# Differential attention in a two-layer trunk: the bias table written reversed for every partition, the softmax turned to minima, one division moved into the output norm

## The chip, the cores and the metric

The kernel runs on one core of a Trainium2 chip. The metric is the device time of one execution in microseconds (us); of several runs the median counts. Inside the core, TensorE (PE) multiplies matrices, VectorE (DVE), ScalarE (ACT) and GpSimd (POOL) work on elements, and SyncE (SP) issues transfers. ACT and POOL issue transfers as well. Every engine takes its instructions in order, and semaphores make one wait for another.

## The reference, cut to what matters

The kernel computes a trunk of two layers on 512 tokens of width 1024: a Mamba-2 mixer, a feed-forward block with a short convolution (FFN 0), a differential attention with a relative-position bias, and a second feed-forward block (FFN 1). The change is in the attention and in the table of its bias:

```python
dist = qpos[:, None] - kpos[None, :]
bias = rel_bias[t5_bucket(dist)].astype(jnp.float32).transpose(2, 0, 1)
logits = jnp.einsum('bqhcd,bkhcd->bhcqk', qblk, k).astype(jnp.float32) * scale
logits = logits + bias[None, :, None]
logits = jnp.where(dist >= 0, logits, -jnp.inf)
p = jax.nn.softmax(logits, axis=-1)
attn = p[:, :, 0] - lam * p[:, :, 1]
return jnp.einsum('bhqk,bkhd->bqhd', attn.astype(v.dtype), v)
...
o = rms_norm(o, subln_g) * (1.0 - lam_init)
```

There are 8 heads with two softmax maps each. The bias depends on the head and on the distance between query and key alone, so that for one head it is a line of 512 numbers that is shifted by one from query to query.

## The kernel before

Products are made in parts: a weight is split into a high part `wh` (rounded, by ACT) and a low part `wl` (the rest, by DVE), and three matmuls take the place of one. `chunk` hands out the next weights of a long plan, two chunks ahead of their use; each chunk is loaded by SP into one of three raw buffers, copied by ACT and subtracted by DVE. A scheduler puts the instructions of every engine in order when the program is built; in the attention, PE's order is the one in which the code is written.

**FFN 0.** Its 22 pairs of column blocks come in three parts (`PARTS_D`: 6, 8 and 8 pairs). Behind the pairs of a part stand the seven products of a Strassen-like down projection, in the order 5, 1, 2, 6, 7, 4, 3 (`SEVEN[0]`), each in two chunks. Their weights are sums of blocks of `ffn_down_w`. `combine` (L1060) makes them: it copies a running sum to `wh` and `wl` (L1074, L1075), and then lets POOL add the next block to that running sum by an accumulating transfer (`plus`, L1046 and L1047). Product 6 needs what is added to `wz` after product 5, product 7 what is added to `wx` after product 1, and product 3 what is added to `wz` after product 6.

**The bias table.** `bias_ranges` (L977) runs in FFN 0 behind pair 3. POOL loads `rel_bias` (`rb`, 8 heads by 32 buckets), spreads it over distances (`bv`, two halves of 320 columns, L990) and writes it to DRAM (`bd`, 8 rows of 640, L991). In POOL's order the writes stand ahead of the accumulating loads for products 6 and 7 of the first part.

**The attention.** The queries of a head are worked on in three units (`PARTS`: blocks 0 and 1, block 2, block 3). `logits` (L1489) loads the bias of a head once: the transfer at L1494 reads the line of `bd` from a start that moves by one from partition to partition into `tr`, and DVE copies it backwards into `tb` (L1495), of which there are two. PE makes the logits (L1508), DVE adds the bias and finds the maximum of each row in one instruction (L1514), turns the sign of the maxima (L1517), and ACT makes the exponentials with that bias and their sums `sm` (L1522). `weigh` (L1525) divides: `rc` holds the inverse of both sums, and the second map is weighted by lambda times the first sum over the second and added to the first. `turn` transposes the result, `values` (L1547) multiplies by the values and lets ACT scale each block by the inverse of the first sum (L1558). `normed_out` (L1561) makes the root-mean-square norm over a head's 128 outputs, `turned_out` transposes them for the output projection. Between all this, PE is fed with pieces of the projections of values, queries and output (`fill`).

Of the kernel before, what the change touches and what calls it, by code (L numbers as in the profile page):

```python
# [9 lines left out]
F32 = mybir.dt.float32  # L10
# [3 lines left out]
ALU = mybir.AluOpType  # L14
# [19 lines left out]
AH = 8  # L34
EPS = 1e-6
NEG = -1.0e30
LAM_INIT = 0.8 - 0.6 * math.exp(-0.3 * 1)
NBIAS = 640

# [2 lines left out]
def trunk_kernel(ctx: ExitStack, tc, x, ssm_ln_g, ssm_in_w, ssm_conv_w, ssm_conv_b, ssm_dt_bias,  # L42
# [416 lines left out]
    def params_a():  # L459
        pin(dve.tensor_copy(st2[64:80, :].rearrange("p (j q) -> p j q", j=2),  # L460
                            d2[64:80, :].unsqueeze(2).to_broadcast([16, 2, 64])))
        param(c2, st2, 80)
        dve.tensor_scalar(out=c2[:, 49:50], in0=c2[:, 49:50], scalar1=64 ** -0.5, scalar2=None, op0=ALU.mult)
        dve.tensor_scalar(out=c2[:, 50:51], in0=c2[:, 50:51], scalar1=1.0 - LAM_INIT, scalar2=None,
                          op0=ALU.mult)

# [20 lines left out]
        dve.scalar_tensor_tensor(out=xgl[k], in0=xT[k], scalar=g, in1=xgh[k].bitcast(F32),  # L487
                                 op0=ALU.mult, op1=ALU.subtract)

    def rsqrt_act(v, pl, name, shape, n):  # L490

        m = pl.tile(shape, F32, tag="rs_m", name="rsm_" + name, bufs=2)
        t = pl.tile(shape, F32, tag="rs_t", name="rst_" + name, bufs=2)
        dve.tensor_scalar(out=m, in0=v, scalar1=1.0 / n, scalar2=EPS, op0=ALU.mult, op1=ALU.add)
        act.activation(v, m, AF.Ln)
        act.activation(v, v, AF.Exp, scale=-0.5)
        dve.tensor_tensor(out=t, in0=v, in1=v, op=ALU.mult)
        dve.scalar_tensor_tensor(out=t, in0=t, scalar=-0.5, in1=m, op0=ALU.mult, op1=ALU.mult)
        dve.scalar_tensor_tensor(out=v, in0=t, scalar=1.5, in1=v, op0=ALU.add, op1=ALU.mult)
# [452 lines left out]
        run(out_proj(NG - 1, *prev, norm))  # L952


    bd = dp.tile([AH, NBIAS], F32, name="bd")
    ks = dp.tile([D, D], F32, name="ks")

    def key_weights(k0, i):
# [18 lines left out]
    def bias_ranges(pl, behind):  # L977
        rb = pl.tile([AH, 32], F32, name="rb")
        pool.tensor_copy(rb[:, 0:1], behind[:AH, 0:1])
        pool.dma_start(rb, rel_bias.rearrange("b h -> h b"))  # L980
        hb = NBIAS // 2
        for i in range(2):
            bv = pl.tile([AH, hb], F32, name="bv%d" % i)
            if i == 0:
                pool.memset(bv[:, 0:P - 1], NEG)
            for b, a, e in _ranges():
                a, e = max(a - i * hb, 0), min(e - i * hb, hb)
                if a < e:
                    src = rb[:, 0:e - a] if b == 0 else rb[:, b:b + 1].to_broadcast([AH, e - a])
                    pool.tensor_copy(bv[:, a:e], src)  # L990
            pool.dma_start(bd[:, i * hb:(i + 1) * hb], bv)  # L991

    def ffn(l, norm, bp, gnext, nnext):
        with tc.tile_pool(name="ffn_h%d" % l, bufs=1) as hp, tc.tile_pool(name="ffn%d" % l, bufs=1) as fp:
# [292 lines left out]
    with tc.tile_pool(name="att", bufs=1) as ap, ExitStack() as later:  # L1287
# [191 lines left out]
        class Unit:  # L1479
# [9 lines left out]
            def logits(self):  # L1489
                h, tag, st = self.h, self.tag, self.st  # L1490
                if self.part == 0:
                    st["tb"] = up.tile([P, T], F32, tag="tb", name="tb%d" % h, bufs=2)
                    tr = up.tile([P, T], F32, tag="tr", name="tr%d" % h, bufs=1)
                    sync.dma_start(tr, bass.AP(tensor=bd.tensor, offset=h * NBIAS, ap=[[1, P], [1, T]]))  # L1494
                    dve.tensor_copy(st["tb"], tr[:, ::-1])  # L1495
                i2, h4 = h // 4, h % 4
                k = len(self.ii)
                mx = up.tile([P, k, 2], F32, tag="mx%d" % k, name="mx" + tag, bufs=3)
                self.sm = up.tile([P, k, 2], F32, tag="sm%d" % k, name="sm" + tag, bufs=3)
                self.p = [up.tile([P, T], F32, tag="p%d" % m, name="lg%s_%d" % (tag, m), bufs=3)  # L1500
                          for m in range(2)]
                pss = [aux_bank("lg%s_%d" % (tag, m)) for m in range(2)]
                for j, i in enumerate(self.ii):
                    n = (i + 1) * P
                    c = slice(self.off[j], self.off[j] + n)
                    for m in range(2):
                        rows = slice(64 * m, 64 * (m + 1))
                        pe.matmul(pss[m][:, c], qT[i2][rows, h4, i * P:(i + 1) * P], kT[i2][rows, h4, :n],  # L1508
                                  start=True, stop=True)
                for j, i in enumerate(self.ii):  # L1510
                    n = (i + 1) * P
                    c = slice(self.off[j], self.off[j] + n)
                    for m in range(2):
                        dve.tensor_tensor_reduce(self.p[m][:, c], pss[m][:, c],  # L1514
                                                 st["tb"][:, (3 - i) * P:], 1.0, -3.0e38,
                                                 ALU.add, ALU.max, mx[:, j, m:m + 1])
                dve.tensor_scalar(out=mx, in0=mx, scalar1=-1.0, scalar2=None, op0=ALU.mult)  # L1517
                for j, i in enumerate(self.ii):
                    n = (i + 1) * P
                    for m in range(2):  # L1520
                        v = self.p[m][:, self.off[j]:self.off[j] + n]
                        act.activation(v, v, AF.Exp, bias=mx[:, j, m:m + 1],  # L1522
                                       accum_out=self.sm[:, j, m:m + 1])

            def weigh(self):  # L1525
                sm, p = self.sm, self.p
                k = len(self.ii)
                rc = self.rc = up.tile([P, k, 2], F32, tag="rc%d" % k, name="rc" + self.tag, bufs=4)
                dve.reciprocal(rc, sm)

                dve.scalar_tensor_tensor(out=sm[:, :, 1:2], in0=sm[:, :, 0:1], scalar=nlam[:, 1:2],
                                         in1=rc[:, :, 1:2], op0=ALU.mult, op1=ALU.mult)
                for j, i in enumerate(self.ii):
                    c = slice(self.off[j], self.off[j] + (i + 1) * P)
                    self.weighed = dve.scalar_tensor_tensor(
                        out=p[0][:, c], in0=p[1][:, c], scalar=sm[:, j, 1:2], in1=p[0][:, c],
                        op0=ALU.mult, op1=ALU.add).ins
# [9 lines left out]
            def values(self):  # L1547
# [4 lines left out]
                for j, i in enumerate(self.ii):  # L1552
                    o = self.off[j]
                    for k in range(i + 1):
                        pe.matmul(ps[:, j * P:(j + 1) * P], self.at[:, o + k * P:o + (k + 1) * P],
                                  vt[k][:, h * P:(h + 1) * P], start=(k == 0), stop=(k == i))
                for j, i in enumerate(self.ii):
                    act.activation(self.st["ot"][:, i, :], ps[:, j * P:(j + 1) * P], AF.Copy,  # L1558
                                   scale=self.rc[:, j, 0:1])

        def normed_out(h, st):  # L1561
            ot = st["ot"]
# [1 line left out]
            so = up.tile([P, NT], F32, tag="so", name="so%d" % h, bufs=2)  # L1564
            act.activation(sq, fl(ot), AF.Square)
            dve.reduce_sum(so, sq.rearrange("p (a q) -> p a q", a=NT), axis=AX.X)
            rsqrt_act(so, ap, "o%d" % h, [P, NT], P)
            dve.tensor_tensor(out=ot, in0=ot, in1=so.unsqueeze(2).to_broadcast([P, NT, P]), op=ALU.mult)

        def turned_out(h, st):  # L1570
# [192 lines left out]
```

## Time and profile before

| | us |
|---|---|
| median of 3 runs | 1318.85 (1318.2 to 1319.2) |
| the profiled execution | 1318.59 |
| its span, first to last instruction | 1316.9 |
| PE busy | 1311.8 |
| DVE, ACT, POOL busy | 1087.6, 719.4, 176.4 |

The granted clock of PE was 1.000 throughout. A group's row gives line, engine, operation, what it writes and reads, its shapes and its count, then busy time in us and the mean of one in ns, then the idle time of that engine just ahead of it with what ended it. A row of busy time by stretch gives the stretch, its length, then the busy time and the count of PE, of its weight loads, of DVE, ACT and POOL, then the granted clock, the busy share of the DMA engines and the GB/s that they moved. A row of the timeline gives start, duration, engine, line, operation and count. Time from issue to landing stands last in a row of transfers.

### The profile page before, as it was taken

The page shows a single profiled execution, that of the slowest core. Times are in us where ns is not written, and L with a number is a line of the kernel's source. Part 1 is how long each engine was busy: PE and PEld are TensorE (multiplying, and loading weights), DVE is VectorE, ACT ScalarE, POOL GpSimd, SP SyncE. Part 2 cuts the span into 40 slices and gives each one's busy share as a digit, 9 for nine tenths or more (in the row PEclk, how much of TensorE's full clock was granted, in tenths as well). Part 3 has the DMA queues.
Part 4 walks back from the last instruction along what each step waited for, and adds up shares of the span by engine and source line. Part 5 has one row for each costly group of instructions (what it writes and reads, how often), then busy time and mean ns, then how long its engine had stood idle before and what let it go on. Part 6 is the DMA issues. An engine that isn't in the chain of part 4 may idle for free.

```text
span 1316.9 us, 18295 instructions
## 1 busy us (share of the span) xinstructions
PE 1311.8 (100%) x6771; PEld 1097.2 (83%) x6771; DVE 1087.6 (83%) x1822; ACT 719.4 (55%) x1170; POOL 176.4 (13%) x243
## 2 busy tenths in 40 slices
PE   9999999999999999999999999999999999999998
PEld 8878888888888988898889887777888888888887
DVE  7889878888878887986889878678778878887886
ACT  6696554743354545544556676777655444544452
POOL 4230200300021401110112310000020100010001
PEclk9999999999999999999999999999999999999999
DMA  7553433532234657673866764221225445443625
GB/s 208 156 152 91 150 100 107 141 95 85 85 96 138 118 147 205 178 161 112 221 162 145 186 135 125 76 65 56 65 80 160 97 119 186 102 96 112 192 64 128
DMA packets 202553, 167.85 MB, mean 127 GB/s; under 512 B 7580, under 2 KB 175904, under 8 KB 202464
## 3 DMA queue, kind: packets, MB, share of 16 engines
q1 hardware_dynamic: 176080, 124.93, 31.9%
q0 software_dynamic: 22928, 36.46, 14.8%
q10 hardware_dynamic: 3456, 5.30, 1.1%
q8 instruction: 53, 0.87, 0.3%
q14 instruction: 36, 0.29, 0.1%
HBM read 160.21 MB, written 6.44 MB: 127 GB/s over the span
## 4 chain that ended last, share of the span: by engine, by line
PE 99%; DVE 0%; issue 0%; ACT 0%; DVEq 0%
PE ps_u L209 6%; PE ps_g L209 6%; PE ps_g L208 6%; PE ps_u L207 6%; PE ps_g L207 6%; PE ps_u L208 6%; PE ps_in L207 5%; PE ps_in L209 5%; PE ps_in L208 5%; PE ps_s L1229 3%; PE ps_s L1232 3%; PE ps_s L1231 3%; PE ps_s L1140 3%; PE ps_s L1135 3%; PE ps_s L1138 3%; PE ps_o L208 2%
## 5 line engine op out<-in xcount | busy, mean ns | idle before, releaser
L207 PE MATMUL ps_u<-xgh,wh_u 128*128 128x512 f32 x352 | 137.4, 390 | 0.0
L207 PE MATMUL ps_g<-xgh,wh_g 128*128 128x512 f32 x352 | 137.0, 389 | 0.0
L209 PE MATMUL ps_u<-xgh,wl_u 128*128 128x512 f32 x352 | 137.0, 389 | 0.0
L208 PE MATMUL ps_g<-xgl,wh_g 128*128 128x512 f32 x352 | 137.0, 389 | 0.0
L209 PE MATMUL ps_g<-xgh,wl_g 128*128 128x512 f32 x352 | 137.0, 389 | 0.0
L208 PE MATMUL ps_u<-xgl,wh_u 128*128 128x512 f32 x352 | 136.9, 389 | 0.0
L207 PE MATMUL ps_in<-xgh,wh_in 128*128 128x512 f32 x304 | 122.9, 404 | 0.0
L209 PE MATMUL ps_in<-xgh,wl_in 128*128 128x512 f32 x304 | 119.7, 394 | 0.0
L208 PE MATMUL ps_in<-xgl,wh_in 128*128 128x512 f32 x304 | 119.2, 392 | 0.0
L208 PEld LDWEIGHTS ps_g<-xgl,wh_g 128*128 128x128 f32 x352 | 66.1, 188 | 13.7
L209 PEld LDWEIGHTS ps_g<-xgh,wl_g 128*128 128x128 f32 x352 | 66.1, 188 | 13.7
L209 PEld LDWEIGHTS ps_u<-xgh,wl_u 128*128 128x128 f32 x352 | 66.0, 188 | 13.7
L1232 PE MATMUL ps_s<-sl,wh_s 128*128 128x256 f32 x308 | 77.5, 283 | 0.0
L1231 PE MATMUL ps_s<-sh,wh_s 128*128 128x256 f32 x308 | 77.5, 283 | 0.0
L207 PEld LDWEIGHTS ps_u<-xgh,wh_u 128*128 128x128 f32 x352 | 66.1, 188 | 13.5
L207 PEld LDWEIGHTS ps_g<-xgh,wh_g 128*128 128x128 f32 x352 | 66.0, 188 | 13.6
L208 PEld LDWEIGHTS ps_u<-xgl,wh_u 128*128 128x128 f32 x352 | 66.1, 188 | 13.6
L1120 ACT ACTIVATE sh<-vg 128x256 fp32r<-128x256 f32 (+1 forms) x44 | 23.0, 524 | 96.6 <-DVE vg L1270 96.5
L1047 POOL DMA_DIRECT2D wz<-in_ffn_down_w_dram x36 | 44.2, 1293 | 233.5 <-DVE wl_s L1075 163.2
L1266 ACT ACTIVATE vg<-vg 128x512 f32<-128x512 f32 x44 | 27.8, 633 | 78.4 <-DVE vg L1019 78.4
L1019 DVE SCALAR_TENSOR_TENSOR vg<-ug,cf,vg 128x511 f32<-128x511 f32 x88 | 65.9, 749 | 5.5 <-ACT vg L1017 4.1
L1016 DVE TENSOR_TENSOR uu<-ps_u,nr_f 128x512 f32<-128x512 f32 x44 | 30.4, 691 | 47.5 <-PE ps_u L209 47.5
(427 smaller groups left out, 3532.2 us busy)
## 6 DMA issues: line engine op xcount, KB each, us to landing
wr_g<-in_ffn_up_w_dram SPq DMA_DIRECT2D x44, 512.0 KB, 3.9
wr_u<-in_ffn_up_w_dram SPq DMA_DIRECT2D x44, 512.0 KB, 3.9
wr_in<-in_ssm_in_w_dram SPq DMA_DIRECT2D x40, 512.0 KB, 3.9
wz<-in_ffn_down_w_dram POOLq DMA_DIRECT2D x27, 512.0 KB, 5.9
m<-cumd POOLq DMA_DIRECT2D x16, 512.0 KB, 4.3
wr_out<-in_ssm_out_w_dram SPq DMA_DIRECT2D x16, 512.0 KB, 3.4
wr_s<-in_ffn_down_w_dram SPq DMA_DIRECT2D x13, 512.0 KB, 3.7
xT<-in_ffn_down_w_dram SPq DMA_DIRECT2D x10, 512.0 KB, 6.9
```

The source lines that it names most:

```text
L207: pe.matmul(ps, wh, xh, start=start, stop=False)
L208: pe.matmul(ps, wh, xl, start=False, stop=False)
L209: return pe.matmul(ps, wl, xh, start=False, stop=stop).ins
L1016: dve.tensor_tensor(out=u, in0=ps, in1=r, op=ALU.mult)
L1019: dve.scalar_tensor_tensor(out=v[:, s:], in0=u[:, :T - s], scalar=col(2 - s), in1=v[:, s:], op0=ALU.mult, op1=ALU.add)
L1047: pool.dma_start(view(t, nq), source(p0, c, nq, j, i), accum_op=ALU.add)
L1135: pe.matmul(pss[b], h, ws[q][1][:, cols], start=False, stop=end and q == qs[-1], skip_group_check=more)
L1138: pe.matmul(pss[b], h, ws[q][0][:, cols], start=first and q == qs[0], stop=False, skip_group_check=more)
L1140: pe.matmul(pss[b], w, ws[q][0][:, cols], start=False, stop=False, skip_group_check=more)
L1229: pe.matmul(v[:, b], wl[:, q, cols], h, start=False, stop=q == nq - 1)
L1231: pe.matmul(v[:, b], wh[:, q, cols], h, start=q == 0, stop=False)
L1232: pe.matmul(v[:, b], wh[:, q, cols], w, start=False, stop=False)
```

## The change

1. **The table is written reversed, and once for each partition.** `bd` grows from 8 x 640 to 8 x 128 x 640 numbers. `bv` holds the line backwards with the sign turned, and each half is written 128 times from the same eight partitions. The load of a head reads rows that are 639 apart, so that the line comes shifted and in the right direction, straight into `tb`; `tr` and the copy go.
2. **Signs are turned.** The scale of the queries is negative, the table is negated by one POOL instruction, the mask is +1e30. DVE finds minima in place of maxima, and these are the bias of the exponentials (with scale -1) without a turn of sign.
3. **The first sum's division goes into the norm.** The outputs are left unscaled, one ACT copy for each unit, and the norm's epsilon is multiplied by the square of the first sum (`eps`). The sums of a head lie in one tile, `sm`.

```diff
-        dve.tensor_scalar(out=c2[:, 49:50], in0=c2[:, 49:50], scalar1=64 ** -0.5, scalar2=None, op0=ALU.mult)
+        dve.tensor_scalar(out=c2[:, 49:50], in0=c2[:, 49:50], scalar1=-(64 ** -0.5), scalar2=None, op0=ALU.mult)
...
-    def rsqrt_act(v, pl, name, shape, n):
+    def rsqrt_act(v, pl, name, shape, n, eps=None):
...
-        dve.tensor_scalar(out=m, in0=v, scalar1=1.0 / n, scalar2=EPS, op0=ALU.mult, op1=ALU.add)
+        if eps is None:
+            dve.tensor_scalar(out=m, in0=v, scalar1=1.0 / n, scalar2=EPS, op0=ALU.mult, op1=ALU.add)
+        else:
+            dve.scalar_tensor_tensor(out=m, in0=v, scalar=1.0 / n, in1=eps, op0=ALU.mult, op1=ALU.add)
...
-    bd = dp.tile([AH, NBIAS], F32, name="bd")
+    bd = dp.tile([AH, P, NBIAS], F32, name="bd")
...
         pool.dma_start(rb, rel_bias.rearrange("b h -> h b"))
+        pool.tensor_scalar(out=rb, in0=rb, scalar1=-1.0, scalar2=None, op0=ALU.mult)
         hb = NBIAS // 2
         for i in range(2):
             bv = pl.tile([AH, hb], F32, name="bv%d" % i)
-            if i == 0:
-                pool.memset(bv[:, 0:P - 1], NEG)
+            if i:
+                pool.memset(bv[:, hb - (P - 1):], FAR)
             for b, a, e in _ranges():
-                a, e = max(a - i * hb, 0), min(e - i * hb, hb)
+                a, e = max(NBIAS - e - i * hb, 0), min(NBIAS - a - i * hb, hb)
                 if a < e:
-                    src = rb[:, 0:e - a] if b == 0 else rb[:, b:b + 1].to_broadcast([AH, e - a])
+                    src = rb[:, 0:e - a][:, ::-1] if b == 0 else rb[:, b:b + 1].to_broadcast([AH, e - a])
                     pool.tensor_copy(bv[:, a:e], src)
-            pool.dma_start(bd[:, i * hb:(i + 1) * hb], bv)
+            pool.dma_start(bd[:, :, i * hb:(i + 1) * hb], bv.unsqueeze(1).to_broadcast([AH, P, hb]))
...
-                    tr = up.tile([P, T], F32, tag="tr", name="tr%d" % h, bufs=1)
-                    sync.dma_start(tr, bass.AP(tensor=bd.tensor, offset=h * NBIAS, ap=[[1, P], [1, T]]))
-                    dve.tensor_copy(st["tb"], tr[:, ::-1])
+                    sync.dma_start(st["tb"], bass.AP(tensor=bd.tensor, offset=h * P * NBIAS + P, ap=[[NBIAS - 1, P], [1, T]]))
+                    st["sm"] = up.tile([P, NT, 2], F32, tag="sm", name="sm%d" % h, bufs=3)
...
-                                                 st["tb"][:, (3 - i) * P:], 1.0, -3.0e38,
-                                                 ALU.add, ALU.max, mx[:, j, m:m + 1])
-                dve.tensor_scalar(out=mx, in0=mx, scalar1=-1.0, scalar2=None, op0=ALU.mult)
+                                                 st["tb"][:, (3 - i) * P:], 1.0, 3.0e38,
+                                                 ALU.add, ALU.min, mx[:, j, m:m + 1])
...
-                        act.activation(v, v, AF.Exp, bias=mx[:, j, m:m + 1],
+                        act.activation(v, v, AF.Exp, bias=mx[:, j, m:m + 1], scale=-1.0,
...
-                rc = self.rc = up.tile([P, k, 2], F32, tag="rc%d" % k, name="rc" + self.tag, bufs=4)
-                dve.reciprocal(rc, sm)
+                dve.reciprocal(sm[:, :, 1:2], sm[:, :, 1:2])
...
-                for j, i in enumerate(self.ii):
-                    act.activation(self.st["ot"][:, i, :], ps[:, j * P:(j + 1) * P], AF.Copy,
-                                   scale=self.rc[:, j, 0:1])
+                k = len(self.ii)
+                act.activation(self.st["ot"][:, self.ii[0]:self.ii[0] + k, :],
+                               ps[:, :k * P].rearrange("p (a d) -> p a d", a=k), AF.Copy)
...
-            rsqrt_act(so, ap, "o%d" % h, [P, NT], P)
+            e = up.tile([P, NT], F32, tag="eps", name="eps%d" % h, bufs=2)
+            s0 = st["sm"][:, :, 0]
+            dve.scalar_tensor_tensor(out=e, in0=s0, scalar=EPS, in1=s0, op0=ALU.mult, op1=ALU.mult)
+            rsqrt_act(so, ap, "o%d" % h, [P, NT], P, e)
```

Three places of the order show what moves. The first is POOL in FFN 0, first part, where the table is written (`bd`) and the running sums `wz` and `wx` are added to. Before:

```order
L990 COPY bv_4063<-rb 8x320
L991 DMA bd<-bv_4043 8x320
L991 DMA bd<-bv_4063 8x320
L1047 DMA wz_0_3661<-in_ffn_down_w_dram 128x3x256
L1047 DMA wz_1_3662<-in_ffn_down_w_dram 128x3x256
L1047 DMA wx_0_3663<-in_ffn_down_w_dram 128x3x256
```

The same place of the changed kernel:

```order
L995 COPY bv_4047<-rb 8x80
L996 DMA bd<-bv_4044 1024x1x320
L996 DMA bd<-bv_4047 1024x1x320
L1052 DMA wz_0_3661<-in_ffn_down_w_dram 128x3x256
L1052 DMA wz_1_3662<-in_ffn_down_w_dram 128x3x256
L1052 DMA wx_0_3663<-in_ffn_down_w_dram 128x3x256
```

The order is the same; each write of the table has 1024 rows of 320 numbers where it had 8.

The second place is PE in the down projection of the same part. `wh_s_0_1_4312` (before) and `wl_s_0_1_4314` (changed) belong to the second chunk of product 2; `wh_s_0_0_4337` and `wh_s_0_0_4338` are the high weights of product 6, copied from `wz`. Before:

```order
L1231 MATMUL ps_s_0_1_4367<-sh_4142,wh_s_0_1_4312 128x256
L1232 MATMUL ps_s_0_1_4367<-sl_4143,wh_s_0_1_4312 128x256
L1231 MATMUL ps_s_0_0_4391<-sh_3772,wh_s_0_0_4337 128x256
L1232 MATMUL ps_s_0_0_4391<-sl_3773,wh_s_0_0_4337 128x256
L1231 MATMUL ps_s_0_0_4391<-sh_3939,wh_s_0_0_4337 128x256
L1232 MATMUL ps_s_0_0_4391<-sl_3940,wh_s_0_0_4337 128x256
L1229 MATMUL ps_s_0_0_4342<-sh_3772,wl_s_0_0_4286 128x256
```

The changed kernel, where product 6 begins:

```order
L1234 MATMUL ps_s_0_1_4368<-sh_3772,wl_s_0_1_4314 128x256
L1234 MATMUL ps_s_0_1_4368<-sh_3939,wl_s_0_1_4314 128x256
L1234 MATMUL ps_s_0_1_4368<-sh_4143,wl_s_0_1_4314 128x256
L1236 MATMUL ps_s_0_0_4392<-sh_3772,wh_s_0_0_4338 128x256
L1237 MATMUL ps_s_0_0_4392<-sl_3773,wh_s_0_0_4338 128x256
L1236 MATMUL ps_s_0_0_4392<-sh_3939,wh_s_0_0_4338 128x256
```

Before, product 6 began ahead of the low parts of product 2; now all of product 2 stands ahead of it. The same matmuls run.

The third place is SP in the attention, from the second load of `q` weights on. Before:

```order
L1494 DMA tr_7838<-bd 128x512
L139 DMA wr_q_4_7756<-in_q_w_dram 128x2x512
L139 DMA wr_q_6_7871<-in_q_w_dram 128x2x512
L1494 DMA tr_8002<-bd 128x512
L139 DMA wr_v_0_7962<-in_kv_w_dram 128x2x512
L139 DMA wr_v_2_8086<-in_kv_w_dram 128x2x512
L1494 DMA tr_8187<-bd 128x512
L139 DMA wr_v_4_8232<-in_kv_w_dram 128x2x512
```

The changed kernel (`tb_7829` is the second head's, `tb_7984` the third's):

```order
L1498 DMA tb_7829<-bd 128x512
L140 DMA wr_q_2_7671<-in_q_w_dram 128x2x512
L140 DMA wr_q_4_7750<-in_q_w_dram 128x2x512
L140 DMA wr_q_6_7858<-in_q_w_dram 128x2x512
L140 DMA wr_v_0_7943<-in_kv_w_dram 128x2x512
L140 DMA wr_v_2_8061<-in_kv_w_dram 128x2x512
L1498 DMA tb_7984<-bd 128x512
L140 DMA wr_v_4_8201<-in_kv_w_dram 128x2x512
```

The load of the third head stands where that of the fourth (`tr_8187`) stood. The weight loads keep their order among themselves.

More of the change, by code (lines that the diff above doesn't have):

```diff
@@ L36 @@
 NEG = -1.0e30
+FAR = 1.0e30
 LAM_INIT = 0.8 - 0.6 * math.exp(-0.3 * 1)
@@ L1498, in logits @@
                 mx = up.tile([P, k, 2], F32, tag="mx%d" % k, name="mx" + tag, bufs=3)
-                self.sm = up.tile([P, k, 2], F32, tag="sm%d" % k, name="sm" + tag, bufs=3)
+                self.sm = st["sm"][:, self.ii[0]:self.ii[-1] + 1, :]
                 self.p = [up.tile([P, T], F32, tag="p%d" % m, name="lg%s_%d" % (tag, m), bufs=3)
@@ L1526, in weigh @@
                 sm, p = self.sm, self.p
-                k = len(self.ii)
-                rc = self.rc = up.tile([P, k, 2], F32, tag="rc%d" % k, name="rc" + self.tag, bufs=4)
-                dve.reciprocal(rc, sm)
+                dve.reciprocal(sm[:, :, 1:2], sm[:, :, 1:2])
                 dve.scalar_tensor_tensor(out=sm[:, :, 1:2], in0=sm[:, :, 0:1], scalar=nlam[:, 1:2],
-                                         in1=rc[:, :, 1:2], op0=ALU.mult, op1=ALU.mult)
+                                         in1=sm[:, :, 1:2], op0=ALU.mult, op1=ALU.mult)
                 for j, i in enumerate(self.ii):
```

## The prediction

> **What bounds the kernel now.** I read the page's busy times and its chain first, then what TensorE (PE) waits for, then busy times by stretch.
>
> ```profile
> span 1316.9 us, 18295 instructions
> PE 1311.8 (100%) x6771; PEld 1097.2 (83%) x6771; DVE 1087.6 (83%) x1822; ACT 719.4 (55%) x1170; POOL 176.4 (13%) x243
> PE 99%; DVE 0%; issue 0%; ACT 0%; DVEq 0%
> ```
>
> PE is busy for 1311.8 of 1316.9 us and makes up 99% of the chain that ended last. The list of what PE waits for, over the whole span, has one row, at the very start. The stretch that holds the attention has no idle PE at all:
>
> ```profile
> PE warm L291 <- DVE ones L218: 1.1, 1, 1.1
> 800.00:950.00 150.00, 150.00 (x829) 115.02 (x828) 114.58 (x358) 106.22 (x274) 0.00 (x0) 1.00 0.22 68
> ```
>
> In the second row the first number is the length and the second PE's busy time. So work taken from VectorE (DVE) or ScalarE (ACT) in the attention cannot shorten the span unless it ends a PE wait, and there is none to speak of. The kernel is fast because every operand is ready in time; an edit can hardly win, but it loses whatever it makes an operand late by. The question is which operand the change makes late.
>
> **The change in the attention: worth nothing.** Groups of DVE and ACT between 790 and 950 us:
>
> ```profile
> L1495 DVE COPY tb<-tr 128x512 f32<-128x512 f32 x8 | 3.4, 422 | 1.1 <-DMA tr<-bd 1.1
> L1517 DVE TENSOR_SCALAR mx<-mx 128x2 f32<-128x2 f32 x16 | 2.7, 168 | 0.4
> L1517 DVE TENSOR_SCALAR mx<-mx 128x4 f32<-128x4 f32 x8 | 1.3, 165 | 0.1
> L499 DVE SCALAR_TENSOR_TENSOR so<-rst_o,so 128x4 f32<-128x4 f32 x8 | 1.3, 159 | 0.1
> L1558 ACT ACTIVATE ot<-po,rc 128x128 f32<-128x128 f32 x32 | 11.0, 362 | 10.7 <-PE po L1555 10.3
> ```
>
> DVE loses the eight reversing copies (3.4 us) and the sign turns (2.7 + 1.3 us). It gains eight small eps products, priced as L499: 8 x 159 ns = 1.3 us. That is 6.1 us less. ACT's 32 output copies become 24; eight of those left out are 8 x 362 ns = 2.9 us, less what eight wider ones cost. All of it lies beside a PE that is busy for 150.00 of 150.00 us, so I price it at nothing. The row of the logits' line bounds a gain from below:
>
> ```profile
> issue: 3.2, 18
> ```
>
> The logits' matmuls and weight loads were held up 3.2 us in all with no releaser that the trace shows; if every bit of it were a DVE step that is now shorter, the gain would be 3.2 us. PE being busy meanwhile, I take 0.
>
> The bias load now lands straight in `tb`, and `tb` of head h has to wait until DVE has read that of head h-2. On SyncE's (SP) queue, weight loads stand behind that wait.
>
> ```profile
> 823.61 0.34 SPq L1494 DMA_DIRECT2D tr<-bd  x1
> 839.93 0.62 SPq L1494 DMA_DIRECT2D tr<-bd  x1
> tr<-bd SPq DMA_DIRECT2D x8, 256.0 KB, 3.3
> ```
>
> The old load of head h had to wait for the copy of head h-1, which DVE made right behind the last logits of head h-3. The new one is due one head later, at the same DVE step as the old load of the next head, so it takes that load's place: 823.61 for the third head, 839.93 for the fourth. The weight loads around them keep their order. It lands 3.3 us later, a head (16.3 us between these rows) ahead of its use. The loads read 2 KB rows before and after. Price 0; if that slack were gone, one landing, 3.3 us, for each of six heads would be the worst.
>
> **The change in the first FFN: a transfer 128 times as large, in front of weights.** The bias table is built on GpSimd (POOL). It was written as 8 rows of 1280 bytes, twice; now it is 1024 rows of 1280 bytes, twice: 2 x 1,310,720 bytes = 2.62 MB, all read from the same eight SBUF partitions. Behind it in POOL's order, and in the same software queue, stand the accumulating loads of the down projection:
>
> ```profile
> 438.74 1.24 POOL L991 DMA_DIRECT2D bd<-bv  x2
> 439.99 2.65 POOL L1047 DMA_DIRECT2D wz<-in_ffn_down_w_dram  x2
> 445.73 1.26 POOL L1047 DMA_DIRECT2D wx<-in_ffn_down_w_dram  x1 [3.08 <-DVE wl_s L1075]
> 449.77 1.26 POOL L1047 DMA_DIRECT2D wx<-in_ffn_down_w_dram  x1 [2.79 <-DVE wl_s L1075]
> ```
>
> The products that use them, in order of time on PE (its first matmul of the down projection) and on ACT (the copies that feed it, one for each chunk):
>
> ```profile
> 443.62 0.28 PE L1231 MATMUL ps_s<-sh,wh_s 128*128 128x256 f32 x1
> ...
> 452.14 0.85 ACT L1074 ACTIVATE wh_s<-wz 128x768 fp32r<-128x768 f32 x1 [0.58 <-ACT sh L1120]
> ...
> 465.04 0.85 ACT L1074 ACTIVATE wh_s<-wz 128x768 fp32r<-128x768 f32 x1 [1.31 <-PE ps_s L1232]
> 467.20 0.85 ACT L1074 ACTIVATE wh_s<-wz 128x768 fp32r<-128x768 f32 x1 [1.31 <-PE ps_s L1232]
> ```
>
> The two `wz` loads make the weights of product 6, the two `wx` loads those of product 7. PE begins the products at 443.62 and takes 467.20 - 465.04 = 2.16 us for a chunk. Product 6 starts with the seventh chunk, in the changed order of PE: 443.62 + 6 x 2.16 = 456.58. Its weights must be copied by ACT first (0.85 us).
>
> What is not in the trace is how long 2.62 MB take from eight partitions. Four rows of busy time and transfer (last number: GB/s) bound it:
>
> ```profile
> 440.55:440.75 0.20, 0.20 (x3) 0.16 (x2) 0.17 (x2) 0.00 (x0) 0.20 (x1) 1.00 0.24 52
> 440.50:440.80 0.30, 0.30 (x3) 0.26 (x2) 0.27 (x2) 0.00 (x0) 0.30 (x1) 1.00 0.16 34
> 442.00:448.00 6.00, 6.00 (x45) 5.70 (x44) 4.18 (x7) 2.96 (x5) 1.90 (x2) 1.00 0.96 137
> 504.00:505.20 1.20, 1.20 (x7) 0.98 (x6) 1.17 (x2) 0.70 (x1) 0.00 (x0) 1.00 1.02 399
> ```
>
> The first two hold the eight rows of the second old `bd` write, the third the `wz` loads on the same queue, the last a store from all 128 partitions (`ks`). At 399 GB/s the new write would take 6.6 us, at 137 GB/s 19.1 us, at 52 GB/s 50.4 us, at 34 GB/s 77 us. I take 52: same eight partitions, same queue, same row size, with the window drawn close around the burst. Its weakness is that eight rows are a short sample, which their start-up may have stretched.
>
> [...]
>
> The sum: POOL gets one instruction more (the sign turn of 8x32, about the 0.4 us of a small copy below), and issuing rises from 549 ns for 8 rows, by the slope of these rows, to about 2 us for 1024.
>
> ```profile
> L990 POOL COPY bv<-rb 8x3 f32<-8x3 f32 (+12 forms) x18 | 5.7, 365 | 5.2 <-DMA rb<-in_rel_bias_dram 5.2
> L991 POOL DMA_DIRECT2D bd<-bv x2 | 1.1, 549 | 0.1
> L1047 POOL DMA_DIRECT2D wz<-in_ffn_down_w_dram x36 | 44.2, 1293 | 233.5 <-DVE wl_s L1075 163.2 <-DMA wz<-in_ffn_down_w_dram 24.5 <-ACT sh L1120 22.7
> ```
>
> (1293 ns for 384 rows or fewer gives (1293 - 549) / 376 = 2 ns a row, so at most 2.6 us.) The write begins at 438.74 + 0.4 + 2.0 = 441.1 and ends at 441.1 + 50.4 = 491.5. The first `wz` (384 KB at 137 GB/s = 2.9 us) lands at 494.4 and is copied by 495.2; PE has waited 495.2 - 456.58 = 38.7 us. Each of the next three chunks then comes 2.9 us after the last where PE needs 2.16: 3 x 0.74 = 2.2 us more. Together 40.9 us. In general the loss is the write's length minus 9.5 us.
>
> After such a pause PE may restart slowly, as at the start of the span, where 18 passes took 4.21 us (234 ns) against 12 in 1.47 us (122 ns) later:
>
> ```profile
> 1.14 4.21 PE L291 MATMUL warm<-ones 128*128 128x128 f32 x18 [1.14 <-DVE ones L218]
> 13.13 1.47 PE L308 MATMUL xgb<-ident,xt 128*128 128x128 f32 x12
> ```
>
> That is 18 x 112 ns = 2.0 us, and the 2.2 us for which PE waits for late chunks cover it; I add nothing. The scheduler also moved product 6's matmuls behind all of product 2's; the same matmuls run, so 0.
>
> The profiled execution took 1318.59 us (its span and 1.7 us around it), 0.26 under the median of 1318.85. 1318.59 + 40.9 = 1359.5.
>
> **The rivals.**
>
> *Wide write (ends on the other side).* The write spreads over the DMA engines as `ks` does; the loss begins only when it lasts over 9.5 us (276 GB/s). At 399 GB/s it lasts 6.6 us and nothing is late: 1318.6 (up to 12 us cost less than the 2.6 us that count as no change). For it: the cover is real. Against it: eight rows together ran at 52, not 399. Chance 0.14. [...]
>
> *Partly wide.* The queue's own rate, 137 GB/s, holds: 19.1 us, a loss of 9.6, 1328.2. With a write of 12 to 45 us the times are 1321 to 1354. Chance 0.13.
>
> *Faster.* Late operands do not occur and the logits' 3.2 us come back: 1315.4. Against it: PE has no idle time there. Chance 0.02.
>
> *Longer still.* At 34 GB/s the write lasts 77 us: 1386. Chance 0.03 of a time above my range.
>
> **How the numbers follow.** The read path gets 0.68: one short burst for it, none against. Its own range: 45 us of writing gives 1354; at the upper end SP's loads into its three raw buffers, filled twice in that time, 6 x 512 KB = 3.1 MB, would go in between at 137 GB/s, 23 us more: 1382. Leaving out the wide write, the faster and the longest case (0.19) gives 1321 to 1382. About 0.2% (2.6 us) is what a measurement here can tell from no change. Slower: 0.68 + 0.13 + 0.03 = 0.84; same 0.14; faster 0.02.
>
> **What would show it.** Right: PE idle for some 40 us in one piece near 457 to 495 us, ACT's copy of `wz` waiting for a DMA there, the two `bd` writes landing some 25 and 50 us after issue, at about 52 GB/s; the attention still without idle PE. Wrong: `bd` landing within 10 us and no gap there; or a gap of another length, which would put the rate wrong and not the mechanism; or gaps in the attention at the bias loads, which I priced at nothing.

## The result and the profile after

| | before | after |
|---|---|---|
| median, us | 1318.85 (1318.2 to 1319.21, 5 runs) | 1362.15 (1360.15 to 1364.09, 5 runs) |
| profiled execution, us | 1318.59 | 1360.15 |
| its span, us | 1316.9 | 1358.4 |

The changed kernel is slower: ratio 1.033, 95% interval 1.0318 to 1.0341, which is 43.3 us between the medians and 41.5 us between the two profiled spans.

The page of the changed kernel: span, busy times, two rows of the forty slices (34 us each; tenths of busy time, and of the granted clock), and the shares of the chain that ended last.

```profile
span 1358.4 us, 18271 instructions
PE 1313.5 (97%) x6771; PEld 1097.8 (81%) x6771; DVE 1084.9 (80%) x1798; ACT 716.0 (53%) x1162; POOL 179.2 (13%) x244
PE   9999999999999449999999999999999999999998
PEclk9999999999999769999999999999999999999999
PE 91%; another core or an unknown queue 3%; DVE 2%; ACT 1%; DMA 1%; issue 1%; DVEq 0%; SPq 0%; ACTq 0%; POOLq 0%
```

PE does the same 6771 matmuls in about the same busy time (1313.5 us), but its share of the chain fell from 99% to 91%. The span is longer by one hole, in the 14th and 15th slices. What PE waits for names it, and the list over all engines names what ACT waited for in turn (columns: us in total, times, longest):

```profile
PE ps_s L1236 <- ACT wh_s L1079: 38.9, 1, 38.9
PE warm L292 <- DVE ones L219: 1.1, 1, 1.1
...
ACT wh_s L1079 <- DMA wz<-in_ffn_down_w_dram: 52.2, 8, 38.5
```

One wait of 38.9 us, for ACT's copy of the weights `wz`, and ACT was waiting for their transfer. GpSimd's row of time shows the issue of the table and of the loads behind it, ACT's the copies that followed:

```profile
431.81 0.32 POOL L985 TENSOR_SCALAR rb<-rb 8x32 f32<-8x32 f32 x1 [5.09 <-DMA rb<-in_rel_bias_dram]
...
437.71 2.21 POOL L996 DMA_DIRECT2D bd<-bv  x2
439.91 2.67 POOL L1052 DMA_DIRECT2D wz<-in_ffn_down_w_dram  x2
```

```profile
494.08 0.84 ACT L1079 ACTIVATE wh_s<-wz 128x768 fp32r<-128x768 f32 x1 [38.54 <-DMA wz<-in_ffn_down_w_dram]
496.98 0.84 ACT L1079 ACTIVATE wh_s<-wz 128x768 fp32r<-128x768 f32 x1 [2.06 <-DMA wz<-in_ffn_down_w_dram]
499.86 0.85 ACT L1079 ACTIVATE wh_s<-wx 128x768 fp32r<-128x768 f32 x1 [2.04 <-DMA wx<-in_ffn_down_w_dram]
502.15 0.84 ACT L1079 ACTIVATE wh_s<-wx 128x768 fp32r<-128x768 f32 x1 [1.44 <-DMA wx<-in_ffn_down_w_dram]
```

The transfers of the changed kernel between 442 and 476 us: `q0` is GpSimd's software queue, and the last number its share of 16 engines' time; below it the median time from issue to landing.

```profile
DMA packets 373, 1.85 MB, mean 54 GB/s; under 512 B 12, under 2 KB 12, under 8 KB 373
...
q0 software_dynamic: 373, 1.85, 96.2%
...
wr_g<-in_ffn_up_w_dram SPq DMA_DIRECT2D x1, 512.0 KB, 46.4
wz<-in_ffn_down_w_dram POOLq DMA_DIRECT2D x1, 384.0 KB, 56.1
wr_s<-in_ffn_down_w_dram SPq DMA_DIRECT2D x1, 384.0 KB, 40.5
```

In these 34 us nothing moved but the table, at 54 GB/s. Note the two loads of SP (`wr_g`, `wr_s`): they stand in another queue and yet took 40 and 46 us; in the same window of the kernel before such loads landed in 4.8 and 3.4 us. Busy time by stretch shows the pause and the restart:

```profile
445.00:450.00 5.00, 5.00 (x44) 5.00 (x44) 5.00 (x10) 2.96 (x5) 2.06 (x2) 1.00 0.96 54
460.00:465.00 5.00, 0.00 (x0) 0.00 (x0) 0.00 (x0) 0.00 (x0) 0.00 (x0) 0.50 0.95 53
...
495.00:500.00 5.00, 5.00 (x26) 5.00 (x27) 1.87 (x2) 0.98 (x2) 1.26 (x1) 0.59 1.19 192
500.00:505.00 5.00, 5.00 (x44) 5.00 (x43) 3.53 (x5) 3.03 (x4) 1.28 (x1) 1.00 0.97 152
```

After the busy times stand the granted clock (1.00, 0.50, 0.59, 1.00), the share of the DMA engines and GB/s. In 495 to 500 us PE counts as busy throughout and does only 26 matmuls, where 44 fit at full clock.

The attention has no hole. Its stretch, and groups of DVE and ACT in it (before, the first group's idle time was 4.9 us):

```profile
845.00:995.00 150.00, 149.91 (x829) 115.27 (x828) 110.18 (x330) 103.79 (x267) 1.38 (x1) 1.00 0.22 67
```

```profile
L1518 DVE CUSTOM_DVE_ANT_0 lg<-lg,tb 128x128 f32<-128x128 f32 (+3 forms) x64 | 29.1, 485 | 11.0 <-PE lg L1512 11.0
L1569 DVE SCALAR_TENSOR_TENSOR eps<-sm 128x4 f32<-128x4 f32 x8 | 1.2, 154 | 0.3 <-ACT lg L1525 0.3
...
L1558 ACT ACTIVATE ot<-po 128x128 f32<-128x128 f32 (+1 forms) x24 | 7.1, 297 | 1.6 <-PE po L1555 1.5
```

DVE lost 3.4 + 4.0 us of copies and sign turns there and gained 1.2 us of `eps`. The time turned into waiting: DVE now waits 11.0 us for PE's logits where it waited 4.9.

### The profile page after: what moved, and what is told of

Read it like the earlier page. It is cut to its first block, busy times and chain, and to the rows that moved or that the text cites. A ratio compares the mean times of both kernels' runs of the same rounds, so it can differ in the third digit from the quotient of the medians.

```text
span 1358.4 us, 18271 instructions
## 1 busy us (share of the span) xinstructions
PE 1313.5 (97%) x6771; PEld 1097.8 (81%) x6771; DVE 1084.9 (80%) x1798; ACT 716.0 (53%) x1162; POOL 179.2 (13%) x244
## 4 chain that ended last, share of the span: by engine, by line
PE 91%; another core or an unknown queue 3%; DVE 2%; ACT 1%; DMA 1%; issue 1%; DVEq 0%; SPq 0%; ACTq 0%; POOLq 0%
PE ps_g L209 6%; PE ps_g L210 6%; PE ps_u L209 6%; PE ps_u L208 6%; PE ps_g L208 6%; PE ps_u L210 6%; PE ps_in L208 5%; PE ps_in L210 5%; PE ps_in L209 5%; PE ps_o L209 2%; PE ps_o L208 2%; PE ps_o L210 2%; PE ps_s L1234 2%; PE ps_s L1143 2%; PE ps_s L1140 2%
## 5 line engine op out<-in xcount | busy, mean ns | idle before, releaser
L1236 PE MATMUL ps_s<-sh,wh_s 128*128 128x256 f32 x308 | 78.6, 286 | 38.9 <-ACT wh_s L1079 38.9
L1236 PEld LDWEIGHTS ps_s<-sh,wh_s 128*128 128x128 f32 x308 | 60.0, 195 | 39.2 <-ACT wh_s L1079 39.1
L1079 ACT ACTIVATE wh_s<-wz 128x1024 fp32r<-128x1024 f32 (+2 forms) x42 | 41.5, 988 | 87.6 <-DMA wz<-in_ffn_down_w_dram 52.2
L1080 DVE TENSOR_TENSOR wl_s<-wz,wh_s 128x1024 fp32r<-128x1024 f32 (+2 forms) x42 | 47.0, 1132 | 47.6 <-ACT wh_s L1079 47.3
```

Source lines behind the costliest of these rows:

```text
L1079: act.activation(wh[:, :n], t[:, :n], AF.Copy)
L1080: state["low"] = dve.tensor_tensor(out=wl[:, :n], in0=t[:, :n], in1=wh[:, :n].bitcast(F32), op=ALU.subtract).ins
L1236: pe.matmul(v[:, b], wh[:, q, cols], h, start=q == 0, stop=False)
```

## The experiments

**Theory:** the whole loss is the table's write, which is slow because it reads eight SBUF partitions (the prediction's read path). **Rivals:** the write is slow for another reason (its many rows); the attention took part in the loss, or hides a gain; the write does harm only because weight loads stand behind it in one queue.

### The attention part alone

Before, with the signs turned, minima and the division in the norm; the table stays one line per head (negated), and `tr` with its backward copy stays.

```diff
+        pool.tensor_scalar(out=rb, in0=rb, scalar1=-1.0, scalar2=None, op0=ALU.mult)
...
-                pool.memset(bv[:, 0:P - 1], NEG)
+                pool.memset(bv[:, 0:P - 1], FAR)
...
-                                                 ALU.add, ALU.max, mx[:, j, m:m + 1])
+                                                 ALU.add, ALU.min, mx[:, j, m:m + 1])
-                dve.tensor_scalar(out=mx, in0=mx, scalar1=-1.0, scalar2=None, op0=ALU.mult)
```

> The changed kernel with the narrow table of before (8 rows a half, forward, but negated) and the load into tr with DVE's reversing copy: the turned signs, the minima and the division in the norm alone. If the whole loss is the table's write: 1318.9 within 0.2% (1316.2 to 1321.5). If the attention has a part in the loss (the changed kernel's median is 2.7 us above my sum): 1320 to 1322. If the shorter DVE steps gain: down to 1315.4.

Measured: 1318.73 us (1318.25 to 1319.04, 11 runs) beside 1318.68 of before on the same chip; ratio 1.0001, interval 0.9992 to 1.001. PE's waits, complete:

```profile
PE warm L292 <- DVE ones L219: 1.1, 1, 1.1
```

This half of the change is worth nothing, neither way.

### The write alone

Before, with each half of the table written a second time, 128 times over, to a DRAM buffer that nothing reads.

```diff
+    wide = dp.tile([AH, P, NBIAS], F32, name="wide")
...
             pool.dma_start(bd[:, i * hb:(i + 1) * hb], bv)
+            pool.dma_start(wide[:, 0:128, i * hb:(i + 1) * hb], bv.unsqueeze(1).to_broadcast([AH, 128, hb]))
```

> The kernel before with one thing added: each half of its table is also written 128 times into a DRAM buffer that nobody reads. If the write alone makes the loss: PE waits some 39 us in the first part of the first FFN, 1358 to 1364. If the changed attention is needed for it: 1319.

Measured: 1362.3 us (1361.56 to 1365.35, 4 runs), ratio 1.0335, interval 1.0322 to 1.0348: the loss of the whole change. PE's longest wait in the profiled execution, which at 1365.35 us was the slowest of the four:

```profile
PE ps_s L1233 <- ACT wh_s L1076: 43.0, 1, 43.0
```

The write alone, put into the old kernel, makes the loss; with the run above, nothing that stands out of the spread of these runs (3.8 us) is left for the rest of the change to explain.

### The same write from more partitions

The changed kernel with the half tables built on 16, 32, 64 or 128 partitions (`rep` 2, 4, 8, 16), each of which writes its share of a head's 128 rows. Bytes, packets, target and queue are the same. A small transfer within SBUF spreads `rel_bias` first, so that the writes are issued some 3 us later (at 440.5 us with 128 partitions).

```diff
-        pool.dma_start(rb, rel_bias.rearrange("b h -> h b"))
+        pool.dma_start(r8, rel_bias.rearrange("b h -> h b"))
+        pool.dma_start(rb, r8.unsqueeze(1).to_broadcast([AH, rep, 32]))
...
-            pool.dma_start(bd[:, :, i * hb:(i + 1) * hb], bv.unsqueeze(1).to_broadcast([AH, P, hb]))
+            pool.dma_start(bd[:, :, i * hb:(i + 1) * hb].rearrange("h (r j) c -> (h r) j c", r=rep),
+                           bv.unsqueeze(1).to_broadcast([AH * rep, P // rep, hb]))
```

> The changed kernel, but the table is built on 128 partitions (each head on 16) and written from there: the same 2048 rows of 1280 bytes to the same places, each partition giving 8 rows a half. It needs one more small transfer first, some 3 us. Read path (the eight partitions hold the write to 53 GB/s): the write goes at 137 to 399 GB/s, 19 to 7 us, and 3 us later; the loss is 0 to 13 us: 1318 to 1331. Row theory (each row to DRAM costs what it costs, wherever it comes from): about 51 us again, 1362.

> The changed kernel, but the two half tables are built on 16 partitions (each head twice) and each partition writes 64 of a head's 128 rows; the same 2.62 MB go to the same place on the same queue. Read path theory (the rate goes with the partitions that are read: 53 GB/s from 8, so 106 from 16): the write lasts 25 us from about 442 us; with the run of 128 partitions (write over at 451 us, 3.1 us lost) and the changed kernel (over at 489.6, 43.3 lost) as the two ends of a line, it is over at 467 and loses 3.1 + 16 x 1.04 = 20 us: 1336 to 1341. PE waits once, 17 to 20 us, for ACT's first copy of wz. Rival, a limit that does not go with the partitions (row size, sharing one target, a queue that is quick only when all 128 partitions are in it): 45 us or more, 1355 to 1362; or, if any spreading frees it, about 1322.

> As the run before it with 32 partitions (each head four times, 32 rows from each partition). Read path theory: 212 GB/s, 12.4 us, over at about 454.5, loss 3.1 + 3.5 x 1.04 = 6.7 us: 1324 to 1327. The rival of a fixed limit: 1355 or more. If the rate were limited by the count of rows and not by the partitions, no change against 16 partitions.

> As before with 64 partitions (16 rows from each). [...] If the rate goes with the number of partitions, 64 give what the queue can take, about 340 GB/s as 128 did: 8 to 9 us, 1321 to 1323. [...]

The stretch from 445 to 450 us, inside the write (with 128 partitions the second half landed 10.4 us after its issue, past 451); the last number is GB/s. With 16, 32, 64 and 128 partitions:

```profile
445.00:450.00 5.00, 5.00 (x44) 5.00 (x43) 5.00 (x9) 2.80 (x4) 1.65 (x3) 1.00 0.99 98
```

```profile
445.00:450.00 5.00, 5.00 (x44) 5.00 (x43) 5.00 (x10) 2.96 (x5) 2.23 (x2) 1.00 0.98 201
```

```profile
445.00:450.00 5.00, 5.00 (x44) 5.00 (x43) 5.00 (x10) 2.84 (x4) 1.99 (x2) 1.00 1.00 206
```

```profile
445.00:450.00 5.00, 5.00 (x44) 5.00 (x43) 5.00 (x11) 2.96 (x5) 2.63 (x3) 1.00 1.02 305
```

| partitions | GB/s | PE's longest wait, us | median, us | above before on the same chip | ratio, interval |
|---|---|---|---|---|---|
| 8 (the change) | 54 | 38.9 | 1362.15 | 43.3 | 1.0318 to 1.0341 |
| 16 | 98 | 17.8 | 1340.26 (4 runs) | 21.4 | 1.0149 to 1.018 |
| 32 | 201 | 5.0 | 1328.23 (4 runs) | 9.4 | 1.0059 to 1.0089 |
| 64 | 206 | 9.0 | 1329.78 (4 runs) | 10.9 | 1.0069 to 1.0099 |
| 128 | 305 | 2.7 | 1321.82 (12 runs) | 3.1 | 1.0015 to 1.0032 |

The rate doubles with the partitions up to 32 (54, 98, 201 GB/s), stays from 32 to 64 (206), and rises again at 128 (305); the loss follows it, except from 32 to 64. The rival of the many rows falls, and so does one of too few engines at work: the share of the DMA engines is 0.96 to 1.02 in all five stretches. 64 partitions run like 32, so the rate does not go by their number alone; what else it goes by was not shown. At 128 the trace shows 305 GB/s here and some 330 between 442 and 446 us. With 32 partitions the expected 1324 to 1327 was missed by 1.2 us: the line through two other runs was too simple there. With 64 the expected 1321 to 1323, which took about 340 GB/s, was missed by 6.8. That 64 lose more than 32 at the same rate is a matter of order, as far as the traces tell. With 64 (and 128) the scheduler put product 6 ahead of the low parts of product 2 again, as before the change, so that PE ran out of work at 453.36 us; with 32 it did these low parts first and ran out at 456.35. ACT's first copy of `wz` began at 461.41 and 460.44.

### A source that is not SBUF

The changed kernel with the eight rows written once to a DRAM buffer, from which one DMA makes the 128 copies.

```diff
-            pool.dma_start(bd[:, :, i * hb:(i + 1) * hb], bv.unsqueeze(1).to_broadcast([AH, P, hb]))
+            pool.dma_start(line[:, i * hb:(i + 1) * hb], bv)
+        pool.dma_start(bd, line.unsqueeze(1).to_broadcast([AH, P, NBIAS]))
```

> The changed kernel, but the eight partitions write their rows once to a small DRAM buffer (as before the change), and one DMA then copies that buffer 128 times from DRAM to the table: 2.62 MB from DRAM to DRAM, no SBUF port read. Read path theory: the copy is not held to 53 GB/s; between 137 and 340 GB/s it takes 8 to 19 us, begins about 3 us later (it waits for the small write), and the loss is 3 to 17 us: 1322 to 1336. Rival, the write side (128 rows of one head into one stretch of DRAM, or this queue): 50 us again, 1360 or more.

Measured: 1328.05 us (4 runs), ratio 1.0072, interval 1.0055 to 1.0089. The copy's stretch, and PE's longest wait:

```profile
445.00:450.00 5.00, 5.00 (x44) 5.00 (x44) 5.00 (x10) 2.71 (x5) 2.35 (x3) 1.00 0.84 251
```

```profile
PE ps_s L1238 <- ACT wh_s L1081: 6.3, 1, 6.3
```

The 251 GB/s are the copy and the `wz` and `wx` loads behind it, which moved beside it; the copy's 2560 KB landed 17.3 us after their issue, 152 GB/s over that time. The same target so took the same bytes in about a third of the time (the two writes of the change landed 52.0 and 50.4 us after issue). So the write side was not the limit; the eight partitions were.

### Another queue, and another time

Three runs ask whether the harm is the queue's order. First, ACT issues the two writes:

```diff
-            pool.dma_start(bd[:, :, i * hb:(i + 1) * hb], bv.unsqueeze(1).to_broadcast([AH, P, hb]))
+            act.dma_start(bd[:, :, i * hb:(i + 1) * hb], bv.unsqueeze(1).to_broadcast([AH, P, hb]))
```

> The changed kernel with the two table writes issued by ACT instead of POOL, so that the accumulating loads are no longer behind them in the same queue. Queue order (the loads wait because they are behind the write in one queue): nothing is late, 1319 to 1324. Busy engines (the write keeps all 16 DMA engines at 0.96 with packets of 1.41 us, and any queue's packets take turns with those): 384 rows over 16 engines are 24 turns of 1.41 us = 34 us for a load, so product 6 is still 20 to 40 us late: 1339 to 1362.

Measured: 1351.04 us (4 runs), ratio 1.0248, interval 1.0234 to 1.0261. ACT itself stood still for 12.2 us, some 4 of them until the first half of the table was built and 8.05 in issuing. PE still waited for `wz`:

```profile
433.03 8.05 ACTq L996 DMA_DIRECT2D bd<-bv  x2
441.18 0.63 ACT L1271 ACTIVATE vg<-vg 128x512 f32<-128x512 f32 x1 [12.20 <-issue]
```

```profile
445.54 1.30 POOL L1052 DMA_DIRECT2D wz<-in_ffn_down_w_dram  x1 [10.32 <-DVE wl_s L1080]
```

```profile
PE ps_s L1236 <- ACT wh_s L1079: 20.9, 5, 14.8
```

With no load behind the write in its queue, 32.4 of the 43.3 us remained. Not all of that need be the write's hold on the engines. Because ACT stood still, its copies of the weights before came late, and GpSimd issued the first `wz` load at 445.54 us, where the change has it at 439.91. And PE's busy time is 8.5 us longer than before (1320.3 against 1311.8): the wait came in pieces (20.9 us in five), and the mean granted clock of the run was 0.99, where that of before was 1.000. Next, the write from GpSimd, as in the change, at another time: behind pair 6, where GpSimd has no load to issue for 20 us.

```diff
-                    if not l and p == 3:
+                    if not l and p == 6:
                         bias_ranges(fp, ga)
```

> The changed kernel with the table built four pairs later, behind pair 6: the write of 2.62 MB from eight partitions begins at about 500 us instead of 440, at the start of the next part of the FFN, where GpSimd has no weight load to issue before 519 and the next down projection is 75 us off. Before the change the loads there move 107 to 138 GB/s on SP's queue. Queue theory (the loss came from the weight loads that stood behind the write in its own queue): nothing is late, 1318 to 1322. Engine theory (a write held to 53 GB/s keeps all 16 DMA engines busy, and the loads of the other queues only get turns between its packets): in 50 us the up projection needs about 6 MB and gets a third to a half of it, so TensorE waits 20 to 45 us, now in many pieces at the up projection's weights: 1340 to 1365.

Measured: 1369.85 us (1367.27 to 1370.73, 4 runs), ratio 1.0389, interval 1.0374 to 1.0405: worse than the change. PE's waits, then the transfers between 505 and 535 us (`q1` is SP's queue):

```profile
PE ps_g L208 <- ACT wh_g L148: 28.5, 1, 28.5
PE ps_s L1236 <- ACT wh_s L1079: 16.4, 2, 13.6
```

```profile
q0 software_dynamic: 310, 1.59, 96.2%
q1 hardware_dynamic: 19, 0.01, 0.1%
...
wr_u<-in_ffn_up_w_dram SPq DMA_DIRECT2D x1, 512.0 KB, 48.4
```

As the whole explanation, the theory of the queue's order falls here: PE starved for `wr_g`, the up projection's weights, which SP loads on its own queue. My rival had a size wrong too: I gave these loads a third to a half of what they need, and they got 0.01 MB in 30 us. They did not take turns; they stood still. Then both at once, the moved write issued by ACT:

```diff
-            pool.dma_start(bd[:, :, i * hb:(i + 1) * hb], bv.unsqueeze(1).to_broadcast([AH, P, hb]))
+            act.dma_start(bd[:, :, i * hb:(i + 1) * hb], bv.unsqueeze(1).to_broadcast([AH, P, hb]))
```

> The run with the table moved behind pair 6, but ACT issues the two writes. Here no load stands behind the write in its own queue in either kernel (GpSimd issues none in that time), so the order in a queue can change nothing. In the earlier run with ACT's queue the write went in packets of 1280 bytes and left room for 88 to 103 GB/s in all. If that, and not the order, was what gained 11 us there, this run gains as much or more against the moved one: 1335 to 1360, less some 10 us that ACT is held while it issues. If the eight partitions hold all queues alike, 1364 to 1375.

Measured: 1351.08 us (4 runs), ratio 1.0247, interval 1.0232 to 1.0262. The same stretch (`q10` is ACT's queue), then the stretch from 500 to 511 us, in which nothing but the table moved, and PE's waits above 2 us:

```profile
q10 hardware_dynamic: 1337, 1.79, 45.4%
q1 hardware_dynamic: 1381, 0.70, 8.3%
```

```profile
DMA packets 440, 0.56 MB, mean 51 GB/s; under 512 B 0, under 2 KB 440, under 8 KB 440
q10 hardware_dynamic: 440, 0.56, 43.2%
```

```profile
PE ps_u L208 <- ACT wh_u L148: 15.2, 1, 15.2
PE ps_g L210 <- DVE wl_g L159: 3.6, 3, 2.5
PE ps_g L208 <- ACT wh_g L148: 3.3, 1, 3.3
PE ps_s L1234 <- DVE wl_s L1080: 2.6, 1, 2.6
```

The write is as slow here (51 GB/s; of the 1.79 MB, 0.26 are `ks`, another store on ACT's queue), but it takes 43% of the engines' time, and SP's loads moved 0.70 MB where they moved 0.01. No GpSimd load stood behind the write, so that for SP's traffic the choice of queue matters by itself.

How much of the 18.8 us that this run saved is the queue's is not shown. PE's waits at the up projection fell only from 28.5 to 22.1 us (15.2 + 3.6 + 3.3). Those at the down projection fell from 16.4 to 2.6, and there the scheduler's order differs as well: with the moved write SP's first loads of `wz` stand behind three loads of `wr_s` and went out at 580.11 us, here they stand ahead of them and went out at 549.60.

Two things differ between the queues. The table's packets are 1280 bytes on ACT's queue and 5120 on GpSimd's, some 1.4 us each. And by their share of the time, the table's packets kept 6.9 of 16 engines busy in the mean on ACT's queue (43.2%), but 15.4 on GpSimd's (96.2%), where in the change's records eight are under way at once until the second write's packets begin to move, and sixteen after that. Some 7 at 51 GB/s against some 15 at 54 puts the limit at the source once more, and it suggests that on ACT's queue the write kept only half of the engines; no run separates this from the length of the packets. How long packets would bring SP's loads so near a standstill was not shown either.

I tried to shorten the packets on GpSimd's queue, by cutting each moved write into four of 80 columns:

```diff
-            pool.dma_start(bd[:, :, i * hb:(i + 1) * hb], bv.unsqueeze(1).to_broadcast([AH, P, hb]))
+            for a in range(0, hb, hb // 4):
+                pool.dma_start(bd[:, :, i * hb + a:i * hb + a + hb // 4],
+                               bv[:, a:a + hb // 4].unsqueeze(1).to_broadcast([AH, P, hb // 4]))
```

> The run with the table moved behind pair 6, but each of its two writes is cut into four of 80 columns (rows of 320 bytes in place of 1280, eight DMAs in place of two); the same bytes, partitions, place and queue. In the moved run SP's loads moved 0.01 MB in the 30 us from 505 to 535 while the write had 96% of the engines' time in packets of 5120 bytes of some 1.4 us. If the loads were shut out by the length of the packets, packets of 1280 bytes let several times more through and the loss falls from 51 to some 25 to 40 us (1345 to 1360). [...]

Measured: 1374.33 us (4 runs), ratio 1.0418, interval 1.0401 to 1.0436. This does not settle it: rows were put together again (between 505 and 535 us 273 packets of over 2 KB for the 1.14 MB of the queue, at most some 4.2 KB each in the mean), so that the length hardly changed; and the table came 9 us later by the new order. SP's queue did move 0.96 MB in these 30 us, of which I estimate 0.55 to lie in a burst from 507 to 509.5 us (156, 311 and 271 GB/s in slices of 0.75 us); why the rest got through beside the table, no run tells.

### The wide write at the other time

The same move, with 128 partitions.

> The same move with the table written from 128 partitions (8 rows from each). By both theories the write is over in 9 to 10 us and no load is needed in that time that is not in its buffer already: 1318 to 1320, no difference from the kernel before, and TensorE's only wait the 1.1 us at the start. If it is over 1321, the 2.6 MB cost something wherever they go, whatever their rate.

Measured: 1321.38 us (1320.43 to 1322.36, 9 runs), ratio 1.0022, interval 1.0012 to 1.0032. PE's two longest waits that the kernel before does not have:

```profile
PE ps_s L1238 <- DVE wl_s L1084: 0.9, 1, 0.9
PE ps_u L210 <- DVE wl_u L159: 0.8, 1, 0.8
```

I expected no difference, and it is 2.9 us: even from 128 partitions the 2.62 MB are not quite free. These two waits are 1.7 of the 2.4 us by which the profiled span is longer; what else belongs to the difference was not tried. No version beat the kernel before.

## Why the prediction was right

The forecast was 1359.5 us; the profiled execution took 1360.15, the median run 1362.15. By its steps:

- **What bounds the kernel** held: no gain from DVE or ACT in the attention, shown by the run with that part alone. ACT saved 3.9 us there (11.0 to 7.1) where I had 2.9.
- **The bias loads** of the third and fourth heads, priced at nothing, stand at 864.28 and 880.24 us, 40.7 and 40.3 behind the two old rows whose places they were said to take.
- **The sign turn** took 0.32 us (0.4 predicted). **The issue** of a write took 2.21 / 2 = 1.1 us, not 2.0: the slope that I drew from load rows was too steep. With an earlier start of POOL, the loads behind were issued at 439.9.
- **The write's rate**, the step I called weakest, held: 54 GB/s against 52, from a burst of eight rows. The runs with wider sources show the reason to be the right one. That the number came so close is partly luck: a window 0.1 us wider around the same burst gave 34.
- **The landing** I had as 25 us for the first half and 50 for the second. That was wrong, if harmless. They landed 52.0 and 50.4 us after issue (median 51.2), and `wz` could only follow when both were through: they ran side by side.

```profile
bd<-bv POOLq DMA_DIRECT2D x2, 1280.0 KB, 51.2
```

- **PE's wait**: 38.9 us, 38.7 predicted. ACT copied `wz` at 494.08 (I had 494.4). That this is so close is luck in part, since two misses cancel: the table was down at 489.7 us, 1.8 ahead of my 491.5, and `wz` landed 4.3 us behind it and not 2.9. The next copies came after 2.90, 2.88 and 2.29 us (2.9 each predicted, against 2.16 needed): 1.6 us in place of 2.2.
- **The restart** was said to cost 2.0 us, covered by the late chunks. At a clock of 0.59, 44 - 26 = 18 matmuls fewer in 5 us are 18 x 5 / 44 = 2.0 us. Size and cover both fit: PE's list has no wait for the three late copies, and together the span grew by 41.5 where I had 40.9.
- **The upper end of the range** let SP's loads go in between the write's packets. The trace shows the opposite: SP's stood still, and the table kept the engines (96.2% of 16 engines' time from 442 to 476 us). The loss was no longer for it, presumably because PE was idle for `wz` anyway; moved to a place where PE lives on SP's loads, the same write cost 51 us, of which 28.5 were one wait for them.

What stays open: the median lies 1.8 us further from before than the profiled run does. Runs of the changed kernel differ by 3.9 us, those of before by 1.0. Some kernels here differ as much (the write alone by 3.8 us, 128 partitions by 6.1), others hardly (16 partitions by 0.9), and what decides it in a single run no trace tells. Nor is it separated how much of the 11 us that ACT's queue saved in the first place came from order, how much from shorter packets or fewer engines held, and how much more it would have been without ACT's standstill.

## What to carry to other kernels

Price a transfer by the partitions that it reads, not by its bytes alone: 2.62 MB took some 50 us from 8 partitions and some 9 from 128. Then look at all queues and not only at the one it stands in, because a slow transfer can keep the engines and hold up loads that have nothing to do with it (here SP's moved 0.01 MB in 30 us). And work taken from an engine that waits for TensorE comes back as waiting: DVE's 6.2 us in the attention did (its wait for the logits went from 4.9 to 11.0).

## What the runs showed of the hardware

- Doubling the source partitions doubled the rate from 8 to 32 (54, 98, 201 GB/s), and not from 32 to 64 (206); 128 gave 305.
- On GpSimd's queue the write from 8 partitions took 96.2% of 16 engines' time, and SP's queue moved 0.01 MB in 30 us. On ACT's queue, at about the same rate (51 against 54 GB/s), it took 43.2%, and SP's moved 0.70 MB. ACT paid with 8.05 us of issuing in which it could do nothing else.
- During the pause the granted clock fell to 0.50, and it was 0.59 in the first 5 us after it, with 26 matmuls in place of 44: an estimated 2.0 us beyond the pause's length.
- Two writes on one queue, issued 1.1 us apart, landed together, 52.0 and 50.4 us after issue, not one after the other.
